# Down projection by seven products: one table for the order of all steps

## The chip, the cores and the metric

The kernel runs on one core of one Trainium2 chip. The metric is the device time of one execution in microseconds. The engines are TensorE (PE in the profile; its weight loads PEld), VectorE (DVE), ScalarE (ACT), GpSimd (POOL) and SyncE (SP), whose queue issues nearly all loads.

## What is computed

Two layers of a trunk over 256 context tokens and 1024 latent tokens. The part that matters here ends each layer, a gated dense network with residual:

```python
h2 = rms_norm(x, norm2_g[l]) * (1.0 + sc2) + sh2
gate, up = jnp.split(h2 @ w_ffn_in[l], 2, axis=-1)
x = x + g2 * ((jax.nn.silu(gate) * up) @ w_ffn_out[l])
```

D_MODEL is 1024 and D_FF 2816. All is float32; the kernel keeps it by splitting each operand into a high and a low part and multiplying three times (low x high, high x low, high x high).

## The kernel before

The tokens stand in three groups `CH`: c = 0, the 256 context tokens, and c = 1 and 2, 512 latent tokens each. The residual is in `xs[c]`, eight tiles of 128 rows. The input of the down projection, 22 tiles of 128 rows, is in DRAM as `FS`, and the projection runs in three parts: four tiles plainly (`ffn_out(0)`, `ffn_out(2)`), sixteen tiles by seven products, and the last two plainly (`ffn_out(NF - 2)`).

The middle part goes through `NC = 4` chunks j of four tiles each. Its 2 x 2 blocks are: two halves of the chunk's rows by the two latent groups on the operand side, two halves of the chunk's rows by two halves of the output rows on the weight side. Seven products replace the eight of the block multiplication: b11, b21, b22 use operands as they are, t1 to t4 use sums of operands, and the weight slabs too are used plainly (`w`) or as sums (`s`). For each chunk there are four slabs m, each giving output tiles m and m + 4; I call one (j, m) a step. A product is six matmuls of 512 columns. The context tokens take an ordinary product (`ctx`, 24 matmuls of 256 columns).

TensorE's order in a step is b21, t2, t1, ctx, t3, b22, then b11 of the next step, then t4. Several products gather in one PSUM bank: b11, t2, t3 and t4 of a step all add to bank a, with an eviction between each two, so t2 may start only when the eviction of b11 has read the bank. Evictions `onto` run on VectorE (five of 512 columns and two of 256 a step), `onto2` on ScalarE (`u`) with the addition to x on GpSimd (two a step).

Beside that run two preparations. For the slabs of the next step (`out_sums`): load to `raw`, split into `w` (ScalarE casts the high part, VectorE subtracts for the low part), form the sums by three GpSimd operations in `raw` itself, split again into `s`. For the next chunk: load b11, b21, b22, c and q (`op_load`, `op_c`), eight operand sums on GpSimd (`op_sum`, into q), splits of the sums tile by tile (`op_t`, operands t1 to t4, each 2 x 128x512) and of the plain operands in place (`op_h`, 128x1024). The operands lie in a ring of 12 places, eight to a chunk, so that some can be written only when the running chunk has last read its own.

The order of all engines in this part is the order in which `out7` issues it, under a manual schedule; what is ahead of it (chunk 0's preparation) is put among the evictions of `ffn_out(2)` by the scheduler. `out7` issues a preparation by `do(at, ...)` at step m = at, and four of them at the first step of the chunk that uses them:

```python
if j and m == 0:
    op_t(j, "t3")
    op_h(j, "b22")
...
if j and m == 0:
    op_t(j, "t4")
```

Of the kernel before, what the change touches and what calls it, by code (L numbers as in the profile page):

```python
# [11 lines left out]
F32 = mybir.dt.float32  # L12
# [7 lines left out]
P = 128  # L20
# [30 lines left out]
def build(tc, d):  # L51
# [60 lines left out]
    queue, ready, steps = [], [], []  # L112
# [62 lines left out]


    def out_sums(src):
        raws = []

        def load():  # L180
            raws.append(raw_slab(src))

        def plain():
            w = wtile()
            split(w[:, 0], w[:, 1], raws[0])
            ready.append(w)
# [7 lines left out]
        def sums_():  # L194
            w = wtile()
            split(w[:, 0], w[:, 1], raws[0])
            ready.append(w)

        steps.append((load, plain, quarters, sums_))

    def want(l):
# [372 lines left out]
    for l in range(DEPTH):  # L574
# [890 lines left out]
        def op_load(j):  # L1465
            f = 4 + 4 * j
            for kind, x, c in (("b11", 0, 1), ("b21", 2, 1), ("b22", 2, 2)):
                ld(operand(j, kind)[:, 1], rows_of(f + x, 2, c))
            qs[j] = [qpool.tile([P, 4, 512], F32, tag="q", bufs=2, name=nm("q")) for _ in range(2)]
            for i in range(2):  # L1470
                nc.sync.dma_start(qs[j][i][:, 0], FS[l][f + i, :, CH[2][0]:])
# [9 lines left out]
        def op_t(j, kind, part=(0, 1)):  # L1481
# [37 lines left out]
        def out1(j, m):  # L1519
            w = ready.pop(0)  # L1520
            pa_ = fpsum(512)
            product(pa_, wq(w, 0), opd(j, "b11"))
            onto(1, m, pa_)
            return w, pa_
# [3 lines left out]
        def out7(j, m, w, pa_):  # L1528
            s_ = ready.pop(0)
            last = (j, m) == (NC - 1, 3)  # L1530
            nj = j + 1 if j + 1 < NC else None
            cur = steps.pop(0) if steps and not last else None

            def do(at, *work):
                if nj and m == at:
                    for x in work:
                        x()

            def ctx():
                pc = psum()  # L1540
# [8 lines left out]
            product(pb, wq(w, 2), opd(j, "b21"))
            if cur:  # L1550
                if steps and (j, m) < (NC - 1, 2):
                    steps[0][0]()
                cur[1]()
            onto(1, m, pb)
            do(0, lambda: op_load(nj))
            product(pa_, wq(s_, 0), opd(j, "t2"), False)
            if cur:
                cur[2]()
            onto2(2, m, pa_)
            product(pc, wq(s_, 3), opd(j, "t1"))  # L1560
            onto(2, m + 4, pc)
            do(1, lambda: op_sum(nj, 1))
            do(2, lambda: op_sum(nj, 4), lambda: op_t(nj, "t2", (0,)))
            do(3, lambda: op_sum(nj, 7))
            if j and m == 0:
                op_t(j, "t3")
                op_h(j, "b22")
            if not last:
                ctx()
            if cur:  # L1570
                cur[3]()
            product(pa_, wq(s_, 1), opd(j, "t3"), False)
            onto2(2, m + 4, pa_)
            do(0, lambda: op_sum(nj, 0))
            do(1, lambda: op_sum(nj, 2), lambda: op_sum(nj, 3))
            do(2, lambda: op_sum(nj, 5), lambda: op_sum(nj, 6))
            do(3, lambda: op_h(nj, "b21"), lambda: op_t(nj, "t1"))
            if j and m == 0:
                op_t(j, "t4")
# [220 lines left out]
```

## Time and profile before

| | us |
|---|---|
| median of 3 runs (3018.08 to 3023.95) | 3021.41 |
| the profiled execution | 3017.62 |
| its span, first to last instruction | 3015.5 |
| TensorE busy | 2871.2 (95%) |
| VectorE / ScalarE / GpSimd busy | 2007.7 / 1210.4 / 998.2 |
| seven-product part, layer 0 (1260.42 to 1479.87) | 219.45 |
| seven-product part, layer 1 (2743.20 to 2964.93) | 221.73 |

In the timeline a row is a run of equal instructions without a gap: start, length, engine, line, operation, output<-inputs, shape, count, and in brackets the idle time just before it with what ended it. A row's length includes the tail of its last instruction, so pitches are read from start to start. Tile names are those of the program: `f` and `ps` are PSUM banks, `ft` the operands, `q` their sums, `raw` the slabs.

### The profile page before, as it was taken

Reading aid. Unit: us, or ns where it says so; the run is one execution under the profiler, and the core shown is the slowest. Engines: PE = TensorE matmul, PEld = TensorE weight load, DVE = VectorE, ACT = ScalarE, POOL = GpSimd, SP = SyncE. Lnnn points to the kernel's source line nnn. Section 1 sums busy time; section 2 is a strip of 40 time slices with the busy share of each in tenths; the row PEclk is TensorE's granted clock in tenths of the full one; section 3 lists DMA queues with packets and bytes.
Section 4 is the critical chain, followed back from the end, with each engine's and each line's share of the span. In section 5 each row is a group of like instructions: output and inputs, shape, how many; then the busy total and the mean of one; then the engine's idle time right before and its main releaser. Section 6 shows DMA issues by size and latency. Waiting matters only on the chain.

```text
span 3015.5 us, 41230 instructions
## 1 busy us (share of the span) xinstructions
PE 2871.2 (95%) x15608; PEld 2452.5 (81%) x15608; DVE 2007.7 (67%) x3157; ACT 1210.4 (40%) x2047; POOL 998.2 (33%) x980
## 2 busy tenths in 40 slices
PE   7999999999999999998999999999999999999997
PEld 4888898888888888877777888888888888887776
DVE  6777787685666554777868677776856533356777
ACT  4523687264223233233442237762622223332342
POOL 1222200035443332376512222001444433315663
PEclk9999999999999999999999999999999999999999
DMA  6576523543333233422235665444434312251212
GB/s 229 155 225 186 175 72 112 180 137 109 124 110 123 91 102 133 147 76 96 91 105 161 206 170 150 107 135 135 149 107 133 101 62 69 69 211 63 91 67 84
DMA packets 164406, 380.63 MB, mean 126 GB/s; under 512 B 20576, under 2 KB 56688, under 8 KB 163952
## 3 DMA queue, kind: packets, MB, share of 16 engines
q1 hardware_dynamic: 119680, 274.00, 29.1%
q0 software_dynamic: 44240, 103.84, 10.2%
q8 instruction: 122, 2.00, 0.3%
q14 instruction: 76, 0.62, 0.1%
q10 hardware_dynamic: 288, 0.16, 0.0%
HBM read 281.97 MB, written 95.95 MB: 125 GB/s over the span
## 4 chain that ended last, share of the span: by engine, by line
PE 66%; DVE 15%; issue 6%; POOL 5%; DMA 4%; ACT 4%; SPq 0%; DVEq 0%; POOLq 0%; ACTq 0%
PE f L1286 30%; PE f L249 15%; PE pa L249 6%; PE pa L489 4%; PE S L429 3%; PE ps L447 3%; DVE w L110 2%; PE ps L249 2%; POOL q L1479 2%; PE ps L967 1%; DVE stt L433 1%; DVE ft L110 1%; DMA x<-XS 1%; ACT E L436 1%; DVE ft L1462 1%
## 5 line engine op out<-in xcount | busy, mean ns | idle before, releaser
L110 DVE TENSOR_TENSOR w<-raw,w 128x1024 fp32r<-128x1024 f32 x278 | 356.2, 1283 | 284.6 <-ACT w L109 284.0
L1286 PE MATMUL f<-h,w 128*128 128x512 f32 x2112 | 506.3, 390 | 1.1 <-ACT pc L1234 1.1
L109 ACT CAST w<-raw 128x1024 fp32r<-128x1024 f32 x278 | 289.8, 1050 | 489.9 <-POOL raw L192 116.6
L1286 PEld LDWEIGHTS f<-h,w 128*128 128x128 f32 x2112 | 392.4, 188 | 82.1 <-ACT pc L1234 1.9
L1286 PE MATMUL f<-ft,w 128*128 128x512 f32 x1344 | 324.5, 396 | 30.3 <-DVE ft L1462 14.8
L1286 PEld LDWEIGHTS f<-ft,w 128*128 128x128 f32 x1344 | 249.6, 190 | 95.0 <-DVE ft L1462 19.9
L1286 PE MATMUL f<-T,w 128*128 128x512 f32 x1080 | 264.8, 394 | 15.0 <-DVE pc L1389 12.0
L1286 PEld LDWEIGHTS f<-T,w 128*128 128x128 f32 x1080 | 201.7, 188 | 65.1 <-DVE pc L1389 16.1
L1227 POOL DMA_DIRECT2D FS<-sg x132 | 72.8, 552 | 541.7 <-DVE sg L1358 222.2
L249 PE MATMUL pa<-h,w 128*128 128x512 f32 (+1 forms) x1296 | 248.4, 352 | 0.8 <-DVE vn L667 0.8
L249 PEld LDWEIGHTS pa<-h,w 128*128 128x128 f32 x1296 | 211.3, 191 | 32.4 <-DVE vn L667 1.0
L489 PE MATMUL pa<-w,h 128*128 128x512 f32 x912 | 218.6, 397 | 12.5 <-DVE w L110 12.0
L433 DVE TENSOR_REDUCE stt<-S 128x1 f32<-128x1280 f32 x128 | 189.9, 1487 | 57.3 <-PE S L429 57.3
L249 PE MATMUL f<-mix,w 128*128 128x512 f32 (+1 forms) x1152 | 225.0, 355 | 0.0
L489 PEld LDWEIGHTS pa<-w,h 128*128 128x128 f32 x912 | 171.9, 191 | 52.8 <-DVE w L110 10.0
L249 PEld LDWEIGHTS f<-mix,w 128*128 128x128 f32 x1152 | 189.8, 189 | 29.5
L436 ACT ACTIVATE E<-S,stt 128x1280 f32<-128x1280 f32 x128 | 170.5, 1332 | 40.9 <-DVE stt L433 40.9
L447 PE MATMUL ps<-vt,pt 128*128 128x128 f32 x1280 | 178.0, 279 | 5.3 <-ACT pt L973 5.2
L249 PE MATMUL f<-ft,w 128*128 128x512 f32 (+1 forms) x864 | 173.7, 362 | 5.7 <-DVE x L1107 5.7
L249 PEld LDWEIGHTS f<-h,w 128*128 128x128 f32 x1392 | 172.7, 192 | 3.3
L249 PE MATMUL f<-h,w 128*128 128x256 f32 x1392 | 174.1, 283 | 0.0
L429 PE MATMUL S<-kb,aq 128*128 128x512 f32 (+1 forms) x624 | 162.7, 377 | 9.7 <-ACT E L436 4.7
(247 smaller groups left out, 4877.4 us busy)
## 6 DMA issues: line engine op xcount, KB each, us to landing
raw<-w_fi SPq DMA_DIRECT2D x112, 512.0 KB, 3.8
ra<-w_adaT SPq DMA_DIRECT2D x96, 256.0 KB, 2.8
FS<-sg POOLq DMA_DIRECT2D x88, 256.0 KB, 2.3
kb<-KS SPq DMA_DIRECT2D x52, 320.0 KB, 6.6
raw<-w_adaT SPq DMA_DIRECT2D x32, 512.0 KB, 4.0
raw<-w_fs SPq DMA_DIRECT2D x32, 512.0 KB, 3.9
ft<-FS SPq DMA_DIRECT2D x32, 512.0 KB, 6.0
raw<-w_in SPq DMA_DIRECT2D x20, 512.0 KB, 3.6
```

Of the source, the lines that this page charges most:

```text
L109: S.copy(hi, src)
L110: V.tensor_sub(lo, src, hi.bitcast(F32))
L249: PE.matmul(ps, lhsT=a, rhs=b, start=(i == 0), stop=(i == n - 1))
L429: PE.matmul(ps[:, o:o + n], lhsT=aq[:, m, q0:q0 + P], rhs=kb[m][1 - p][:, o:o + n], start=(p == 0), stop=(p == 1))
L433: V.reduce_max(st[:, m:m + 1], ps[:, :nkey], axis=AX.X, negate=True)
L436: S.activation(E, ps[:, :nkey], AF.Exp, bias=st[:, m:m + 1], accum_out=st[:, 2 + m:3 + m])
L447: PE.matmul(o[:, :P], lhsT=pt[:, i * P:(i + 1) * P], rhs=vt(b + i), start=(b + i == 0), stop=(b + i == nk - 1))
L489: PE.matmul(ps, lhsT=a[:, y], rhs=wk[:, z], start=(k == 0 and x == 0), stop=(k == KD - 1 and x == 2))
L967: PE.transpose(T_["tp", b][:, x * P:(x + 1) * P], T_["E"][0][:, (4 * b + x) * P:(4 * b + x + 1) * P], ident)
L1227: nc.gpsimd.dma_start(FS[l][f, :, t0:t0 + n], sg)
L1286: PE.matmul(ps, lhsT=y, rhs=z, start=(first and i == 0), stop=(i == 3 * len(a) - 1), skip_group_check=not first)
L1479: G.tensor_sub(q[:, o], x, y)
```

## The change

One table, `PLAN`, has four rows, one for each m, and names every step of every engine in the order in which it is issued. The sign behind a name says for which step or chunk it is: `+` the next step, `++` and `+++` those behind it, `-` the one before; `:` the next chunk, `;` the one after. Names: `ld` load of a slab, `r0` to `r3` its sums, `wa`/`wd` the ScalarE and VectorE halves of the split of the plain slab, `sa`/`sd` of the sums; `P1` to `P5` and `C0`, `C1` VectorE's evictions (`P1` that of b11, ahead of t2), `U2`, `U3` ScalarE's with GpSimd's additions `A2`, `A3`; `b21L` and the like loads, `q0` to `q7` operand sums, `t1a`/`t1d` and `b21a`/`b21d` the ScalarE and VectorE halves of an operand's split.

Slab sums go to a tile `s` of their own (one buffer) in four GpSimd operations of 256 elements, and are made two steps ahead; the raw slab stays whole. An operand sum of both tiles is split at once, 128x1024. q is one tile for both. The buffers of `u` are two in place of four. Loads of b11 and b21 are issued two chunks ahead. The two last w_fo slabs go through the same table, and the last two `tf` tiles are split inside it. TensorE's order is as before, apart from the context product of the very last step.

```diff
-        def quarters():
-            r = raws[0].rearrange("p (q c) -> p q c", q=4)
-            G.tensor_add(r[:, 3], r[:, 1], r[:, 3])
-            G.tensor_sub(r[:, 0:2], r[:, 3:4].to_broadcast([P, 2, 256]), r[:, 0:2])
-            G.tensor_sub(r[:, 1:3], r[:, 1:3], r[:, 0:1].to_broadcast([P, 2, 256]))
...
-            for i in part:
-                split(t[:, 0, i], t[:, 1, i], qs[j][i][:, {"t1": 0, "t3": 1, "t2": 2, "t4": 3}[kind]])
...
+            q = qs[j][:, :, SUMS[kind]]
+            if part == "a":
+                S.copy(t[:, 0], q)
+            else:
+                V.tensor_sub(t[:, 1], q, t[:, 0].bitcast(F32))
...
+        def w_load(g):
+            j, m = divmod(g, 4)
+            raws[g] = raw_slab(d["w_fs"][l, j, m] if j < NC else d["w_fo"][l, (4 + m) * P:(5 + m) * P])
+
+        def w_sum(g, n):
+            if not n:
+                sums_[g] = qpool.tile([P, 4, 256], F32, tag="s", name=nm("s"))
+            r, s_ = raws[g].rearrange("p (q c) -> p q c", q=4), sums_[g]
+            if n == 0:
+                G.tensor_add(s_[:, 3], r[:, 1], r[:, 3])
+            elif n == 1:
+                G.tensor_sub(s_[:, 0], s_[:, 3], r[:, 0])
+            elif n == 2:
+                G.tensor_sub(s_[:, 1], r[:, 0], r[:, 1])
+            else:
+                G.tensor_sub(s_[:, 2], r[:, 2], s_[:, 0])
+
+        def w_split(key, src, part):
+            if part == "a":
+                slabs[key] = wtile()
+                S.copy(slabs[key][:, 0], src)
+            else:
+                V.tensor_sub(slabs[key][:, 1], src, slabs[key][:, 0].bitcast(F32))
...
+        def steps(j, loads=None):
+            for m, names in enumerate(PLAN):
+                for name in names.split():
+                    kind = name.rstrip("+-.:;")
+                    sign = name[len(kind):]
...
+                    g = 4 * j + m + len(sign) * (-1 if "-" in sign else 1)
...
+                    step(kind, g)
...
-        op_load(0)
-        op_c(0)
+        steps(-2, True)
+        steps(-1, True)
         ffn_out(2, fds[1])
...
+        steps(-2, False)
+        steps(-1, False)
+        with tc.manual_schedule():
+            for j in range(NC):
+                steps(j)
...
+    """b21 P1 wa+ P4- r0++ t2a: t2 wd+ q3: t1 P2 U2 ld+++ q7: t2d: cx P5 A2 b21d: r1++ t3 C0 r2++ C1 b22
+    r3++ b22d: U3 A3 b11+ sa++ P3 t4 sd++ cL:""",
```

What the table does to the order, at three places of layer 0. In the names, `x_10332`, `x_10336` and `x_10328` are the residuals of groups 1, 2 and 0, `f_` and `ps_` PSUM banks, `ft_` places of the operand ring, `q_` operand sums, `w_` split slabs.

VectorE before, from the last step of chunk 1 (P3) over the turn to chunk 2 (the second row is P1, the eviction of chunk 2's first b11):

```order
L1506 SCALAR_TENSOR_TENSOR x_10336<-f_11567,mod_83,x_10336 128x512
L1506 SCALAR_TENSOR_TENSOR x_10332<-f_11652,mod_83,x_10332 128x512
L1506 SCALAR_TENSOR_TENSOR x_10332<-f_11548,mod_83,x_10332 128x512
L1462 TENSOR_TENSOR ft_10367<-ft_10367 128x1024
L110 TENSOR_TENSOR w_11679<-raw_11574,w_11679 128x1024
L1506 SCALAR_TENSOR_TENSOR x_10332<-f_11669,mod_83,x_10332 128x512
L1506 SCALAR_TENSOR_TENSOR x_10336<-f_11670,mod_83,x_10336 128x512
L110 TENSOR_TENSOR ft_10367<-q_11270,ft_10367 128x512
L110 TENSOR_TENSOR ft_10367<-q_11271,ft_10367 128x512
L1462 TENSOR_TENSOR ft_10367<-ft_10367 128x1024
```

The splits of c, t3 and b22 stand here behind the turn, inside the step that multiplies by them. VectorE after, the same place:

```order
L1462 TENSOR_TENSOR ft_10367<-q_11273,ft_10367 128x1024
L1511 SCALAR_TENSOR_TENSOR x_10336<-f_11598,mod_83,x_10336 128x512
L1462 TENSOR_TENSOR ft_10370<-q_11273,ft_10370 128x1024
L1469 TENSOR_TENSOR ft_10367<-ft_10367 128x1024
L1511 SCALAR_TENSOR_TENSOR x_10328<-ps_11613,mod_83,x_10328 128x256 x2
L1511 SCALAR_TENSOR_TENSOR x_10336<-f_11598,mod_83,x_10336 128x512
L1462 TENSOR_TENSOR ft_10370<-q_11273,ft_10370 128x1024
L1511 SCALAR_TENSOR_TENSOR x_10332<-f_11661,mod_83,x_10332 128x512
L1511 SCALAR_TENSOR_TENSOR x_10332<-f_11556,mod_83,x_10332 128x512
L1497 TENSOR_TENSOR w_11670<-s_11582,w_11670 128x1024
```

Now t3, t1, c and t4 (the four rows that write `ft_`) are split ahead of P1 of the next chunk (the third row from the end), and behind it only slabs are.

VectorE before, in step m = 2 of chunk 1, from P2 to P1 of the next step:

```order
L1506 SCALAR_TENSOR_TENSOR x_10332<-f_11462,mod_83,x_10332 128x512
L1506 SCALAR_TENSOR_TENSOR x_10336<-f_11463,mod_83,x_10336 128x512
L110 TENSOR_TENSOR ft_10367<-q_11270,ft_10367 128x512
L1506 SCALAR_TENSOR_TENSOR x_10328<-ps_11498,mod_83,x_10328 128x256 x2
L110 TENSOR_TENSOR w_11525<-raw_11373,w_11525 128x1024
L1506 SCALAR_TENSOR_TENSOR x_10336<-f_11463,mod_83,x_10336 128x512
L1462 TENSOR_TENSOR ft_10369<-ft_10369 128x1024
L1506 SCALAR_TENSOR_TENSOR x_10332<-f_11548,mod_83,x_10332 128x512
```

P1, the last row, stands behind the split of b11 of the next chunk. VectorE after, the same step:

```order
L1511 SCALAR_TENSOR_TENSOR x_10332<-f_11471,mod_83,x_10332 128x512
L1462 TENSOR_TENSOR ft_10367<-q_11273,ft_10367 128x1024
L1511 SCALAR_TENSOR_TENSOR x_10336<-f_11493,mod_83,x_10336 128x512
L1469 TENSOR_TENSOR ft_10369<-ft_10369 128x1024
L1511 SCALAR_TENSOR_TENSOR x_10328<-ps_11507,mod_83,x_10328 128x256 x2
L1469 TENSOR_TENSOR ft_10367<-ft_10367 128x1024
L1511 SCALAR_TENSOR_TENSOR x_10336<-f_11493,mod_83,x_10336 128x512
L1497 TENSOR_TENSOR w_11563<-s_11482,w_11563 128x1024
L1511 SCALAR_TENSOR_TENSOR x_10332<-f_11556,mod_83,x_10332 128x512
```

Now P1 stands behind the split of the slab sums of two steps ahead (sd), and the step splits three whole operands, t2, b21 and b22.

GpSimd before, in step m = 2 of chunk 1 (the sums of the next slab, additions to x and operand sums):

```order
L190 TENSOR_TENSOR raw_11373<-raw_11373 128x256
L191 TENSOR_TENSOR raw_11373<-raw_11373 128x512
L192 TENSOR_TENSOR raw_11373<-raw_11373 128x512
L1512 TENSOR_TENSOR x_10336<-x_10336,u_11485 128x512
L1479 TENSOR_TENSOR q_11271<-ft_10367,q_11271 128x512
L1512 TENSOR_TENSOR x_10336<-x_10336,u_11534 128x512
L1479 TENSOR_TENSOR q_11271<-q_11271,ft_10369 128x512
L1479 TENSOR_TENSOR q_11271<-ft_10367,q_11271 128x512
```

The slab's sums are one block, in the slab itself. GpSimd after, the same step:

```order
L1484 TENSOR_TENSOR s_11482<-raw_11402 128x256
L1452 TENSOR_TENSOR q_11273<-ft_10369,q_11273 128x512 x2
L1586 TENSOR_TENSOR x_10336<-x_10336,u_11501 128x512
L1486 TENSOR_TENSOR s_11482<-s_11482,raw_11402 128x256
L1488 TENSOR_TENSOR s_11482<-raw_11402 128x256
L1490 TENSOR_TENSOR s_11482<-raw_11402,s_11482 128x256
L1586 TENSOR_TENSOR x_10336<-x_10336,u_11553 128x512
```

Now they are four short operations of the slab two steps ahead, with two operand sums and an addition between them; one operand sum fewer stands in this step and one more in the step ahead of it.

## Rows read from the trace of the kernel before

**Rows 1.** Busy us (count) by stretch: PE, PEld, DVE, ACT, POOL; granted clock, DMA share, GB/s.

```profile
1260.42:1316.68 56.26, 53.45 (x277) 44.87 (x276) 35.26 (x45) 19.14 (x24) 36.20 (x28) 1.00 0.32 109
1316.68:1373.45 56.77, 52.43 (x264) 43.70 (x264) 40.84 (x49) 21.55 (x28) 39.66 (x28) 0.97 0.25 86
1373.45:1429.95 56.50, 51.28 (x264) 42.57 (x264) 41.34 (x49) 21.51 (x28) 39.74 (x28) 1.00 0.22 76
1429.95:1479.87 49.92, 48.02 (x253) 40.66 (x254) 38.64 (x44) 19.06 (x23) 23.68 (x17) 1.00 0.22 68
...
2743.20:2964.93 221.73, 205.71 (x1058) 171.81 (x1056) 157.26 (x186) 80.17 (x102) 138.53 (x101) 0.99 0.24 80
...
1200.00:1230.00 30.00, 30.00 (x158) 25.79 (x157) 21.99 (x31) 9.44 (x10) 4.08 (x4) 1.00 0.91 341
```

**Rows 2.** Timeline of PE in the first chunk of layer 0, undisturbed.

```profile
1266.29 3.04 PE L249 MATMUL ps<-ft,w 128*128 128x256 f32 x24
1269.16 9.71 PE L1286 MATMUL f<-ft,w 128*128 128x512 f32 x42
1278.70 3.04 PE L249 MATMUL ps<-ft,w 128*128 128x256 f32 x24
```

**Rows 3.** Timeline of PE at the turn from the second chunk to the third.

```profile
1357.89 3.06 PE L1286 MATMUL f<-ft,w 128*128 128x512 f32 x12 [0.93 <-DVE x L1506]
...
1370.93 1.43 PE L1286 MATMUL f<-ft,w 128*128 128x512 f32 x5 [1.42 <-DVE ft L1462]
...
1383.06 8.38 PE L1286 MATMUL f<-ft,w 128*128 128x512 f32 x35 [1.27 <-DVE ft L1462]
```

**Rows 4.** PE's waits in 1260.42 to 1479.87: us in total, times, longest.

```profile
PE f L1286 <- DVE ft L1462: 7.7, 6, 1.5
PE f L1286 <- DVE x L1506: 5.1, 5, 1.1
PE f L1286 <- DVE ft L110: 1.1, 2, 0.5
```

**Rows 5.** Timeline of DVE, POOL and ACT in layer 0's part.

```profile
1355.95 1.23 DVE L1462 TENSOR_TENSOR ft<-ft 128x1024 fp32r<-128x1024 f32 x1 [2.21 <-POOL q L1479]
1357.09 0.74 DVE L1506 SCALAR_TENSOR_TENSOR x<-f,mod,x 128x512 f32<-128x512 f32 x1
...
1336.28 1.29 POOL L192 TENSOR_TENSOR raw<-raw 128x512 f32<-128x512 f32 x1
1337.61 1.06 ACT L109 CAST w<-raw 128x1024 fp32r<-128x1024 f32 x1 [3.40 <-POOL raw L192]
1338.70 1.23 DVE L110 TENSOR_TENSOR w<-raw,w 128x1024 fp32r<-128x1024 f32 x1
1338.78 2.30 POOL L1479 TENSOR_TENSOR q<-q,ft 128x512 f32<-128x512 f32 x1
```

**Rows 6.** One stretch by tile: raw, q (DVE, ACT, POOL), u (ACT, POOL), line L1462 (DVE).

```profile
1388.34:1414.82 26.48, 5.72 (x4) 3.15 (x3) 6.95 (x6) 1.00 0.25 82
...
1388.34:1414.82 26.48, 0.73 (x1) 0.61 (x1) 12.83 (x7) 1.00 0.25 82
...
1388.34:1414.82 26.48, 2.76 (x4) 5.16 (x4) 1.00 0.25 82
...
1388.34:1414.82 26.48, 1.23 (x1) 1.00 0.25 82
```

**Rows 7.** POOL's groups in 1260.42 to 1479.87: busy us, mean ns, idle before, releaser.

```profile
L1512 POOL TENSOR_TENSOR x<-x,u 128x512 f32<-128x512 f32 x32 | 44.3, 1384 | 18.4 <-ACT u L1511 18.4
...
L190 POOL TENSOR_TENSOR raw<-raw 128x256 f32<-128x256 f32 x15 | 11.1, 738 | 51.0 <-DVE w L110 51.0
```

**Rows 8.** Timeline of SP's queue ahead of the x loads of layer 0.

```profile
1188.87 0.33 SPq L105 DMA_DIRECT2D raw<-w_fo  x1
1196.38 0.33 SPq L105 DMA_DIRECT2D raw<-w_fs  x1
```

**Rows 9.** PE's waits in 1199 to 1260.42, as in rows 4.

```profile
PE f L249 <- DVE x L1107: 2.9, 2, 2.1
```

More of the change, by code (lines that the diff above doesn't have):

```diff
@@ L110, in split @@
         V.tensor_sub(lo, src, hi.bitcast(F32))
-    queue, ready, steps = [], [], []
+    queue, ready = [], []
     pools = {}
@@ L1462, in halve, with op_load, q_load @@
             V.tensor_sub(t[:, 1], t[:, 1].bitcast(F32), t[:, 0].bitcast(F32))
[L1465 to L1471, printed above, removed]
+        HALVES = {"b11": (0, 2, 1), "b21": (2, 2, 1), "b22": (2, 2, 2), "c": (0, 4, 0)}
+        SUMS = {"t1": 0, "t3": 1, "t2": 2, "t4": 3}
+        def op_load(j, kind):
+            x, n, c = HALVES[kind]
+            ld(operand(j, kind)[:, 1], rows_of(4 + 4 * j + x, n, c))
+        def q_load(j, i):
+            if not i:
+                qs[j] = qpool.tile([P, 2, 4, 512], F32, tag="q", name=nm("q"))
+            nc.sync.dma_start(qs[j][:, i, 0], FS[l][4 + 4 * j + i, :, CH[2][0]:])
         def op_sum(j, n):
             i, n = divmod(n, 4)
-            q = qs[j][i]
+            q = qs[j][:, i]
             b11, b21, b22 = (ops[j, k][:, 1, i].bitcast(F32) for k in ("b11", "b21", "b22"))
@@ L1517, in opd @@
             return [(t[:, 0, i], t[:, 1, i]) for i in range(2)]
[L1519 to L1540, printed above, removed]
+        banks = {}
@@ L1549, in out7 @@
[L1549 to L1579, printed above, removed]
-            product(pc, wq(s_, 2), opd(j, "b22"), False)
-            onto(2, m, pc)
-            do(2, lambda: op_h(nj, "b11"))
-            nxt = None
-            if last:
-                ctx()
-            else:
-                nxt = out1(j, m + 1) if m < 3 else out1(nj, 0)
-            do(2, lambda: op_c(nj), lambda: op_t(nj, "t2", (1,)))
@@ L1656, in build @@
         ffn_out(0, fds[0])
-        op_load(0)
-        op_c(0)
+        steps(-2, True)
+        steps(-1, True)
         ffn_out(2, fds[1])
-        for n in range(8):
-            op_sum(0, n)
-        for kind in ("b11", "b21", "t2", "t1", "c", "t3", "b22", "t4"):
-            (op_t if kind[0] == "t" else op_h)(0, kind)
-        for x in steps.pop(0):
-            x()
-        steps[0][0]()
-        nxt = out1(0, 0)
-        man = ExitStack()
-        man.enter_context(tc.manual_schedule())
-        for j in range(NC):
-            for m in range(4):
-                nxt = out7(j, m, *nxt)
-            if j == NC - 2:
-                for x in range(2):
-                    ld(tf[:, x, 1], FS[l][NF - 2 + x])
-        man.close()
+        steps(-2, False)
[3 more added lines that the diff above has]
+                steps(j)
+            for m, names in enumerate(PLAN):
+                for name in names.split():
+                    if name[-1] == "-" and m < name.count("-"):
+                        step(name.rstrip("-"), 4 * NC + m - name.count("-"))
+        ready.extend(slabs["f", x] for x in range(2))
         fts = [tf[:, x] for x in range(2)]
-        for x in fts:
-            halve(x)
         dq.close()
```

142 lines of the change are left out of this document (110 added, 32 removed).

## The prediction

> **What bounds the kernel now.** I began with the stage that the change touches: the down projection by seven products, once per layer. The table of busy time by stretch [rows 1] cuts it into its four chunks. In layer 0 they take 56.26, 56.77, 56.50 and 49.92 us, together 219.45; the whole stage of layer 1 takes 221.73. Next I asked for TensorE's own timeline. Where nothing stops it [rows 2], 42 matmuls of 512 columns (seven products) go from 1269.16 to 1278.70, 9.54 us or 1.363 per product, and the context product from 1266.29 to 1269.16, 2.87. One step (chunk j, slab m) is therefore 12.41 us at least, a chunk 49.6, and the sixteen steps of a stage 198.6. The change leaves the matmuls as they are, so 198.6 is a floor, and what can be won is 219.45 - 198.6 = 20.9 in layer 0 and 221.73 - 198.6 = 23.1 in layer 1, 44.0 in all. The fourth chunk stands at its floor already; all of the excess lies in the first three.
>
> Where it lies there: at the turn from one chunk to the next TensorE stops four or five times [rows 3]. Product t2 waits for VectorE's eviction of the product before it from the same bank (1357.89). Others wait for an operand that is still being split (1370.93, 1383.06). The list of waits over the stage [rows 4] names the same three: 7.7, 5.1 and 1.1 us, all on VectorE. The rest of the 20.9 is the clock (the second chunk's granted clock is 0.97 on average [rows 1], some of it at the lower of the two levels, 1.2 in place of 2.4 GHz: 0.03 x 56.77 = 1.7 us are lost) and the gaps of some tenths of a microsecond around each stop.
>
> Why VectorE is late: it isn't short of time (41.34 of 56.50 us in the third chunk [rows 1]), it waits in its queue. At 1355.95 the split of b21 has stood idle 2.21 us for a GpSimd sum that reads b21, and the eviction behind it starts at 1357.09 only [rows 5]; t2 follows at 1357.89. And the splits of t3 and b22 are written in the code after the step m = 0 that uses them has begun.
>
> **The change, part by part.** *Order of the operand work.* The splits of b11, b21, b22, t2, t1, t3 and c of the next chunk all stand ahead of the turn in the table, and t4 at the very end of m = 3, a step before its use. The waits for operands (7.7 + 1.1 [rows 4]) then have no cause. *Splits of both tiles at once.* Eight 128x512 splits (0.73 us for the one in [rows 6]) become four 128x1024 at 1.23 [rows 5]: 5.84 to 4.92 us of VectorE per chunk. *Slab sums in a place of their own.* Three GpSimd operations (0.73 + 1.29 + 1.29) become four of 256 elements, 2.92 us in place of 3.31. More important, before, the first of them overwrites the raw slab and must wait for the slab's plain split: GpSimd sat idle 51.0 us of the stage there [rows 7]. That wait goes, and sums are made two slabs ahead. *Evictions* (28 per chunk of VectorE, 8 of ScalarE and GpSimd) stay as they are, as does the last step apart from its context product, which moves up two places.
>
> *The new queueing.* What is late next? VectorE and GpSimd get in each other's way. At 1338.70 a split of 1.23 us runs, and the GpSimd operation that starts 0.08 later takes 2.30 in place of 1.29 [rows 5]; beside evictions, whose first input is in PSUM, I found no such lengthening. So I add for each step what VectorE's operations with two SBUF inputs and GpSimd's would take one after the other. GpSimd has per step 2.92 of sums and 2.58 of additions to x, and of the eight operand sums (1.29) two, four, two, none; VectorE has 3, 3, 5, 5 splits of 1.23:
>
> m = 0: 8.08 + 3.69 = 11.77. m = 1: 10.66 + 3.69 = 14.35. m = 2: 8.08 + 6.15 = 14.23. m = 3: 5.50 + 6.15 = 11.65. Chunk: 52.0, against 49.6 of TensorE.
>
> How much of this fits into a microsecond is read from the busiest stretch of before, 1388.34 to 1414.82, where TensorE stood only at the very end [rows 6]. GpSimd did 17 operations (two of them short: 2 x 0.73 + 15 x 1.29 = 20.81), VectorE 5 x 1.23 + 0.73 = 6.88; together 27.69 us of work in 26.48, or 1.046 per us. GpSimd was idle 1.6 us of it; without these it is 27.69 / 24.84 = 1.115. A whole chunk (52.0 / 49.6 = 1.048) thus just fits. But steps m = 1 and 2 bring 28.58 in a time of 24.82. At 1.046 that needs 27.3, 2.5 too much; at 1.115 it needs 25.6, 0.8 too much. This lateness reaches TensorE by one way: r3 (last slab sum) - sa (ScalarE's half of the split) - sd (VectorE's half) - P1, the eviction behind sd in VectorE's queue - t2 of the next step. Undisturbed, b22 ends 9.68 into a step, sa takes 1.06 more [rows 5], sd 1.23, P1 0.74, so P1 is done at 12.71; t2 wants it at 12.41 + 1.36 = 13.77. Slack 1.06. The stall is then 2.5 - 1.06 = 1.4 or nothing (0.8 < 1.06), once per chunk, and is worked off in m = 3 and 0. I take 1.0, nearer to the first, since GpSimd also waits in order for ScalarE's u (18.4 us of a stage before [rows 7]). Chunks 0 to 2: 50.6; chunk 3, with no operand sums: 49.6; stage 201.4. Gain 219.45 - 201.4 = 18.0 and 221.73 - 201.4 = 20.3; sum 38.3.
>
> This is the place for a rule. In [rows 5] the two operations of 1.23 and 1.29 were over 2.38 us after the first began, not 2.52, so the trace nearly serialises them. The Trainium skill, "SBUF — State Buffer", section "SBUF: two separate sides", says that a GpSimd operation and a VectorE operation with two SBUF inputs exclude each other for the whole instruction. By that rule a chunk could never be under 52.0, a stage would be 205.6, and the gain 30.0; the trace differs by the 1.046 per us above, 5% past what the rule allows, and decides.
>
> *Loads and what lies before the stage.* The order of SP's queue changes: b11 and b21 of chunk 1 (512 KB each) are issued before the x loads, in a gap in which SP stood still anyway, from 1188.87 to 1196.38 [rows 8]. Cost nothing; if that cover were gone, 1 MB more ahead of x costs some 3 us per layer (x and its neighbours moved at 341 GB/s in 1200 to 1230 [rows 1]). The operand work of chunk 0 is still scheduled among the evictions of the product before it, where TensorE waits 2.9 us [rows 9]; the sums that these splits wait for are as many and start on the same load, so I leave it at 2.9, with ends of 0 and 5.8: 3 us per layer either way. What follows the stage I leave as it is. The stretch at the lower clock came after the stage's first stalls, and the third and fourth chunks, with stalls as long, show 1.00; I count it gone. If it stays, it costs 1.7 us per layer.
>
> **The rivals.**
> 1. *All of it is hidden.* GpSimd is always ready and the 1.115 holds; stages at 198.6, gain 44.0, 2977.4. For: 51 us of GpSimd's idle time go. Against: the local 28.58 in 24.82.
> 2. *Strict exclusion*, two-input operations of VectorE and GpSimd never beside each other at all: chunks 52.0, stage 3 x 52.0 + 49.6 = 205.6, gain 30.0, 2991.4. For: 2.30 in place of 1.29. Against: 27.69 in 26.48. (It is the rule named above.)
> 3. *The pair does no better than it did over whole chunks.* Before, a chunk held 12 x 1.23 + 8 x 0.73 + 4 x 0.73 + 24 x 1.29 = 54.5 in 56.50, 0.964 per us. At that rate 52.0 needs 53.9, a stage is 211.3, the gain 18.6: 3002.8. Against: at the turns of before it was the order that held both.
> 4. *Slower.* The stall sits in every step, not once a chunk: the sums have a single tile, so r0 of the next slab waits for sd, and lateness passes from step to step along r3 - sa - sd - P1. Slower from 44.0 / 32 = 1.4 us per step. At 2.2 (m = 1 and 2 overfull by 1.9 and 1.8, and none of it worked off) it would be 70 us of stalls: 3048. Against: m = 0 and 3 have room, 11.8 and 11.7 against 12.4.
> 5. *It doesn't do what it says*: the turns keep their waits because the loads of the next chunk (b22, q, c) come late behind SP's waits for slabs. Gain under 6. Against: the table issues each a half step (6 us) or more before the first instruction that reads it.
>
> **How the numbers follow.** The profiled execution took 3017.62 us, 2.1 more than its span, and lies 3.8 below the median of 3021.41. All terms are differences within the trace, so I take them from the median: 3021.4 - 38.3 = 2983.1. Forecast 0.50, own range 2978 to 2991 (a stall of 0 to 2.4 per chunk). Rivals: all hidden 0.20, strict 0.12, no better than before 0.10, slower 0.05, no effect 0.03. The range leaves out the slower case, the no-effect case and the edges: 2975 (all hidden with 2.5 won before the stage) to 3003. A measurement of this kernel can tell about 0.2%, 6 us, from no change. Faster by more 0.91, within 0.03, slower 0.06.
>
> **What would show it.** Right: the list of waits of TensorE in the stage has no operand splits any more, and one wait of about 1 us per chunk for the eviction P1, at t2 of step m = 3; GpSimd's first slab sum has lost its idle time; stages of 200 to 203 us. Rival 2 or 3: VectorE's splits and GpSimd's operations lengthen further than 1.3 to 1.8 us, with stalls at most steps m = 2 and 3. Wrong: TensorE waiting for ScalarE's u or a slab split, for operand loads, or more than 6 us before the stage.

## The result and the profile after

The changed kernel takes **2982.27 us** (median of 4 runs, 2981.57 to 2983.71); the kernel before, on the same chip, 3022.52 (3018.08 to 3023.95). The ratio is 0.987, with a 95% interval of 0.9853 to 0.9887: faster by 1.3%, clear of the noise. The forecast was 2983.1, with a range of 2975 to 3003.

The profiled execution took 2982.61 us, 35.0 less than the profiled execution of before; its span is 2980.8, 34.7 less. Its stages first. The view is the table of busy time by stretch, as in [rows 1]: the four chunks of layer 0, then the whole stage of layer 1.

```profile
1260.96:1310.35 49.39, 49.13 (x260) 41.81 (x259) 40.09 (x44) 20.15 (x23) 39.67 (x32) 1.00 0.24 74
1310.35:1360.74 50.39, 50.15 (x266) 42.88 (x265) 40.66 (x45) 21.62 (x24) 41.52 (x33) 1.00 0.29 95
1360.74:1411.11 50.37, 50.13 (x266) 42.88 (x265) 40.63 (x45) 21.63 (x24) 41.46 (x33) 1.00 0.27 85
1411.11:1463.53 52.42, 51.53 (x271) 43.89 (x270) 31.95 (x42) 18.29 (x20) 18.73 (x17) 1.00 0.22 76
2726.59:2929.23 202.64, 200.98 (x1058) 171.46 (x1056) 153.15 (x172) 80.65 (x90) 140.18 (x112) 1.00 0.24 77
```

The stages take 202.57 and 202.64 us (forecast 201.4; before 219.45 and 221.73). The gains are 16.9 and 19.1, together 36.0. Before, the first three windows were the long ones; now it is the fourth. The windows are not cut at whole chunks, though, which have 264 matmuls: the fourth here holds 271, seven or some 1.6 us more, and the fourth of [rows 1] 253, some 2.5 us fewer, so that two stops of the kernel before lie inside that one (TensorE's timeline):

```profile
1437.32 0.96 PE L1286 MATMUL f<-ft,w 128*128 128x512 f32 x3 [0.55 <-DVE ft L110]
1439.55 8.66 PE L1286 MATMUL f<-ft,w 128*128 128x512 f32 x35 [1.27 <-DVE ft L1462]
```

Below, steps are compared instead. The granted clock is 1.00 in all of them, so the stretch at the lower level is gone, as I had counted.

TensorE's waits: first those of layer 0's stage, which answer to [rows 4] (layer 1 has the same line), then those before it, which answer to [rows 9].

```profile
PE f L1255 <- DVE x L1511: 1.6, 5, 0.5
...
PE f L218 <- DVE x L1076: 1.8, 2, 1.4
```

No operand split is named any more; the only wait is the one for an eviction. Before the stage 1.8 us are left of 2.9. Line numbers have moved: 1255 is the product (1286 before), 1511 the eviction (1506), 218 the other matmuls (249).

GpSimd's groups in layer 0's stage, as in [rows 7] (busy us, mean ns, idle before, releaser):

```profile
L1586 POOL TENSOR_TENSOR x<-x,u 128x512 f32<-128x512 f32 x32 | 47.8, 1494 | 34.3 <-ACT u L1583 34.3
...
L1486 POOL TENSOR_TENSOR s<-s,raw 128x256 f32<-128x256 f32 x14 | 18.5, 1319 | 0.9
...
L1484 POOL TENSOR_TENSOR s<-raw 128x256 f32<-128x256 f32 x14 | 10.3, 738 | 34.4 <-DVE w L1497 34.4
```

The 51.0 us of idle time ahead of the first slab sum have not gone, they became 34.4: it now waits for the single tile `s`, until VectorE has split the sums in it. But the wait costs nothing now: the kernel with both late edits, near the end of the experiments, idles 37.3 us at the same place of layer 0's stage, and TensorE doesn't wait in that stage at all.

In what follows a step is measured from the start of one context product to the start of the next: 15 steps of a stage, whose floor is 186.3 us (189.0 where the last context product stands two products later, as in the old frame). What a kernel takes above the floor is its **excess**. Before: 20.3 and 21.0 us in the two layers. After: 3.9 and 3.9, of which in layer 0 0.9 lie in the first chunk, 0.7 each in the second and third (at the ends of steps m = 1 and 2, ahead of t2 of the next step), and 1.5 in the fourth (0.78 and 0.72).

### The profile page after: what moved, and what is told of

Read it like the earlier page. It is cut to its first block, busy times and chain, and to the rows that moved or that the text cites. A ratio compares the mean times of both kernels' runs of the same rounds, so it can differ in the third digit from the quotient of the medians.

```text
span 2980.8 us, 41280 instructions
## 1 busy us (share of the span) xinstructions
PE 2867.1 (96%) x15608; PEld 2454.1 (82%) x15608; DVE 2004.4 (67%) x3125; ACT 1210.3 (41%) x2015; POOL 1008.2 (34%) x1012
## 4 chain that ended last, share of the span: by engine, by line
PE 69%; DVE 13%; POOL 6%; issue 5%; ACT 4%; DMA 3%; SPq 0%; DVEq 0%; ACTq 0%; POOLq 0%
PE f L1255 28%; PE f L218 18%; PE pa L218 6%; PE pa L458 4%; PE ps L416 4%; PE S L398 4%; PE ps L218 2%; POOL q L1452 2%; PE ps L936 2%; DVE stt L402 1%; DVE w L110 1%; ACT E L405 1%; POOL x L1586 1%; DVE ps L275 1%; DMA raw<-w_adaT 1%
## 5 line engine op out<-in xcount | busy, mean ns | idle before, releaser
L110 DVE TENSOR_TENSOR w<-raw,w 128x1024 fp32r<-128x1024 f32 x210 | 265.5, 1266 | 270.3 <-ACT w L109 269.8
L109 ACT CAST w<-raw 128x1024 fp32r<-128x1024 f32 x210 | 218.4, 1050 | 356.2 <-POOL raw L159 107.3
L1255 PE MATMUL f<-ft,w 128*128 128x512 f32 x1344 | 315.5, 391 | 3.3 <-DVE x L1511 3.1
L1255 PEld LDWEIGHTS f<-T,w 128*128 128x128 f32 x1080 | 201.7, 188 | 65.4 <-DVE pc L1358 16.1
```

The lines of the kernel that those rows point to most:

```text
L109: S.copy(hi, src)
L110: V.tensor_sub(lo, src, hi.bitcast(F32))
L1255: PE.matmul(ps, lhsT=y, rhs=z, start=(first and i == 0), stop=(i == 3 * len(a) - 1), skip_group_check=not first)
```

## Experiments

**Which part of the change pays?** Two kernels each make one part in the code of before, and one makes both. In the first the slab sums get a tile of their own and become four short operations, in the old order:

```diff
-            G.tensor_add(r[:, 3], r[:, 1], r[:, 3])
...
+            s_ = pools["s"].tile([P, 4, 256], F32, tag="s", name=nm("s"))
+            G.tensor_add(s_[:, 3], r[:, 1], r[:, 3])
...
-            t = qpool.tile([P, 512], F32, tag="u", bufs=4, name=nm("u"))
+            t = qpool.tile([P, 512], F32, tag="u", bufs=2, name=nm("u"))
```

> The kernel before with one part of the change alone: slab sums in a tile of their own (four short GpSimd operations, u with two buffers), everything in the old order. If the order of the operand splits is what pays (my theory), the turns keep their stops and at most the wait of P1 behind a split that waits for GpSimd shrinks: 3012 to 3022. If it is the 51 us of GpSimd's idle time, that is the in-place sums, that held the kernel before: 2992 or less.

Measured: 2995.43 us, ratio 0.9911 (0.9896 to 0.9925); 27.7 us below before. My expectation fell, and the other one (2992 or less) was nearly reached. Excess 8.1 and 8.3. The tile, the shorter operations (2.92 us a step in place of 3.31) and the two buffers of `u` in place of four were not tried apart from each other.

In the second the operand sums and splits move to the steps in which the table has them, and the slab sums stay in the slab:

```diff
-            do(2, lambda: op_sum(nj, 4), lambda: op_t(nj, "t2", (0,)))
-            do(3, lambda: op_sum(nj, 7))
-            if j and m == 0:
-                op_t(j, "t3")
-                op_h(j, "b22")
+            do(1, lambda: op_sum(nj, 1), lambda: op_sum(nj, 5))
+            do(2, lambda: op_t(nj, "t2"))
+            do(3, lambda: op_t(nj, "t3"))
...
-            do(2, lambda: op_sum(nj, 5), lambda: op_sum(nj, 6))
-            do(3, lambda: op_h(nj, "b21"), lambda: op_t(nj, "t1"))
-            if j and m == 0:
-                op_t(j, "t4")
+            do(1, lambda: op_sum(nj, 2))
+            do(2, lambda: op_h(nj, "b21"))
+            do(3, lambda: op_t(nj, "t1"), lambda: op_h(nj, "c"))
...
```

> The kernel before with the operand work alone put where the table has it (operand sums 2, 4, 2, 0 in steps m = 0 to 3; b11 in m = 1; t2, b21, b22 in m = 2; t3, t1, c, t4 in m = 3), slab sums still in place and one step ahead, splits still tile by tile. My theory: most of the 40 us, 2986 to 3000, with what remains as waits for P1, since the two-input work of VectorE and GpSimd is 54.5 per chunk in place of 52.0. If the sums' own place is needed: 3010 or more.

Measured: 3014.21 us, ratio 0.9974 (0.9963 to 0.9985). Excess 17.5 and 16.1. This fell too, and the other expectation (3010 or more) came: where I had put nearly all of the gain there are 9 us. The waits of TensorE, VectorE and GpSimd in layer 0's stage:

```profile
PE f L1286 <- DVE x L1506: 9.7, 8, 2.3
PE f L1286 <- ACT u L1511: 3.1, 3, 1.1
...
DVE w L110 <- ACT w L109: 12.5, 9, 2.8
...
POOL raw L190 <- DVE w L110: 55.1, 12, 6.7
```

The order alone does take away TensorE's waits for operand splits (7.7 + 1.1 us in [rows 4]). But GpSimd still stands 55.1 us ahead of its first slab sum, VectorE 12.5 us at slab splits, and TensorE now waits 9.7 us for evictions in place of 5.1, and 3.1 us for ScalarE's `u`.

> The two parts of e1_own_place and e2_order together. What then separates it from the changed kernel is the split of both tiles at once and that slab sums are one step ahead in place of two. My theory: 2982 to 2990. If the early slab sums carry a part: 2992 to 3005.

Measured: 3006.27 us, ratio 0.9949 (0.9934 to 0.9964); excess 14.5 and 14.1. Both parts together are worse than the first alone, and past both expectations. So the parts don't add up, and "the order" is not one thing. Three traces say what happens. The first lines below are those of the kernel with the own place alone, in layer 0: GpSimd's first slab sum, VectorE's waits for operand sums, and TensorE's waits.

```profile
L192 POOL TENSOR_TENSOR s<-raw 128x256 f32<-128x256 f32 x14 | 15.6, 1117 | 0.0
...
DVE ft L1466 <- POOL q L1483: 3.7, 3, 1.2
...
PE f L1289 <- DVE x L1510: 5.0, 3, 1.7
PE f L1289 <- DVE ft L110: 0.2, 1, 0.2
```

GpSimd no longer idles before a slab sum (51.0 us in [rows 7]); its operand sums come earlier, and VectorE waits 3.7 us for them in place of 9.3 in the stage of before, where [rows 5] show one such wait:

```profile
DVE ft L1462 <- POOL q L1479: 9.3, 6, 2.2
```

TensorE is left with one stop of 1.7 us per turn. The late splits of t3 and b22, written behind the turn, cost 0.2 us in all in that order: they had been late because GpSimd was.

With both parts, the end of step m = 2 looks like this (timeline of layer 0; in the last row TensorE). The slab sums start at 1347.08, behind a run of four operand sums:

```profile
1347.08 1.19 POOL L192 TENSOR_TENSOR s<-raw 128x256 f32<-128x256 f32 x1
...
1350.83 1.05 ACT L109 CAST w<-s 128x1024 fp32r<-128x1024 f32 x1 [4.34 <-POOL s L195]
...
1351.91 1.23 DVE L110 TENSOR_TENSOR w<-s,w 128x1024 fp32r<-128x1024 f32 x1 [2.10 <-ACT w L109]
...
1353.44 1.94 DVE L1466 TENSOR_TENSOR ft<-ft 128x1024 fp32r<-128x1024 f32 x1 [0.30 <-ACT ft L1465]
...
1355.96 1.21 DVE L1466 TENSOR_TENSOR ft<-ft 128x1024 fp32r<-128x1024 f32 x1
...
1357.09 1.39 DVE L1510 SCALAR_TENSOR_TENSOR x<-f,mod,x 128x512 f32<-128x512 f32 x2
...
1357.88 4.62 PE L1289 MATMUL f<-ft,w 128*128 128x512 f32 x12 [2.16 <-DVE x L1510]
```

VectorE stands 2.10 us at the split of the slab sums; behind it in its queue are the splits of b21 and b22 and only then P1 (1357.09), for which t2 waits.

I took that for the cause, and moved the split of the slab sums to the end of the step in this kernel, behind the splits of b21 and b22:

```diff
-            if cur:
-                cur[3]()
...
             do(2, lambda: op_h(nj, "b22"))
+            if cur:
+                cur[3]()
             nxt = None
```

> The combination of the two parts in the old frame (3006.27, step m = 2 stops 2.0 to 2.3 us at t2 of the next step), with one thing moved: both halves of the split of the slab sums go from the middle of the step (behind the context product) to its end, behind the operand splits of the step and ahead of P1. Theory: in the combination VectorE takes that split first, stands 2.10 us for it, and the two operand splits and P1 queue up behind; with the late one last the stop of step m = 2 falls under 1, three times 1.3 to 2.2 us in each of two stages, and the time to 2991 to 2999. Rival: the slab sums themselves are late (GpSimd takes the operand sums first), so the order on VectorE moves the wait without shortening it: 3003 to 3009.

Measured: 3016.03 us, ratio 0.9986 (0.9976 to 0.9996), excess 18.3 in both layers: 10 us worse, and past the rival's figures too. VectorE and ScalarE in the same place:

```profile
1355.38 0.69 ACT L1515 ACTIVATE u<-f,mod 128x512 f32<-128x512 f32 x1 [3.93 <-PE f L1289]
...
1355.96 1.99 ACT L1465 CAST ft<-ft 128x1024 fp32r<-128x1024 f32 x2
1357.09 2.06 DVE L1466 TENSOR_TENSOR ft<-ft 128x1024 fp32r<-128x1024 f32 x1 [2.03 <-POOL x L1516]
```

VectorE now stands at b21's split. GpSimd's addition is named, but ScalarE's halves of the splits of b21 and b22 (1355.96) fit better: the first of the two ends about 1 us in, at 1357. They had stood behind the eviction U3, for whose product ScalarE waited 3.93 us. The stop only changed its place in the queues.

**What of the table makes the difference?** Four of the things that set the changed kernel apart from the kernel with both parts were each taken back alone. Splits of t tile by tile, 128x512 again:

```diff
-                V.tensor_sub(t[:, 1], q, t[:, 0].bitcast(F32))
+                    V.tensor_sub(t[:, 1, i], q, t[:, 0, i].bitcast(F32))
```

> The changed kernel with one part undone: the splits of t1 to t4 tile by tile again (eight of 128x512 in place of four of 128x1024). It adds 0.9 us of VectorE's two-input work per chunk, in steps m = 2 and 3. My theory: it adds to the lateness of P1 at m = 3, 0.2 to 0.9 us per chunk, 2983 to 2988. Rival, that VectorE has room for it: 2982.

Measured: 2986.31 us (2983.25 to 2988.4), 4.0 more than after; the steps that end in m = 3 lengthen from 12.9 or 13.0 us to between 13.2 and 13.7, and the excess is 5.6 and 6.5 in place of 3.9. That is as expected: 0.92 us more of VectorE's work per chunk, on the chain to P1.

Slab sums and splits one step ahead in place of two (`r0++` becomes `r0+` and so on, at the same places; `sd+` of the next chunk's first step moves from behind t2 to the end of m = 3):

```diff
-    b11+ sa++ A3 P3 t4 sd++ q6:""",
+    b11+ sa+ A3 P3 t4 sd+ q6:""",
...
-    b11L; b22 U3 b21L; C0 C1 A3 b11+ P3 t4a: sa++ t4 t4d:""",
+    b11L; b22 U3 b21L; C0 C1 A3 b11+ P3 t4a: sa+ t4 sd+ t4d:""",
```

> The changed kernel with the slab sums and their splits one step ahead in place of two, at the same places of the table (only in the last step of a chunk the second half of the split moves up from behind t2 of the next step). Theory: two steps ahead buy nothing, since with one tile for the sums the chain r3, sa, sd, P1 is the same; 2979 to 2986. Rival: the distance is what lets the crowded steps pass; t2 then waits for its slab at every step, 2990 to 3020.

Measured: 2988.04 us, ratio 0.9894 (0.9879 to 0.9909), 6 more than after and between the two expectations. Away from the turn the distance is worth nothing here: no step there is longer than in the changed kernel. The stop is at the turn (steps of 13.8 us in place of 12.42), and it is the one line that had to move:

```profile
1362.67 1.23 DVE L1497 TENSOR_TENSOR w<-s,w 128x1024 fp32r<-128x1024 f32 x1 [1.22 <-ACT w L1495]
1363.81 1.22 DVE L1462 TENSOR_TENSOR ft<-q,ft 128x1024 fp32r<-128x1024 f32 x1
...
1364.95 2.06 DVE L1511 SCALAR_TENSOR_TENSOR x<-f,mod,x 128x512 f32<-128x512 f32 x3
...
1365.75 3.02 PE L1255 MATMUL f<-ft,w 128*128 128x512 f32 x12 [1.07 <-DVE x L1511]
```

VectorE stands 1.22 us at that split, t4's split and P1 behind it, and TensorE stops for 1.07.

ScalarE's halves of the splits of b21 and b22 back from m = 0 to m = 2, next to VectorE's:

```diff
-    """b21 b11a: P1 qL0: qL1: b22L: P4- wa+ t2 sd+ b21a: t1 P2 r0++ U2 wd+ r1++ cx A2 P5 ld+++ b22a: r2++
+    """b21 b11a: P1 qL0: qL1: b22L: P4- wa+ t2 sd+ t1 P2 r0++ U2 wd+ r1++ cx A2 P5 ld+++ r2++
...
+    r3++ b22a: b22d: U3 A3 b11+ sa++ P3 t4 sd++ cL:""",
```

> The changed kernel with ScalarE's halves of the splits of b21 and b22 moved from step m = 0 to a place right ahead of their VectorE halves in m = 2; nothing else. Theory: ScalarE's lead of two steps is what the old frame lacks (there, in the combination with the split last, the split of b21 on VectorE stood 2.03 us until ScalarE, which works in order behind a u, had done its half); VectorE then waits in m = 2 ahead of P1, the stop at t2 of m = 3 grows from 0.5 to 1.5 to 2.5, and the time to 2989 to 2997. Rival: ScalarE has room there, and the lead is worth nothing: 2980 to 2986.

Measured: 2983.20 us (2981.47 to 2984.32); no change, and the waits of TensorE are the same 1.6 us. In this frame the lead is worth nothing. Here both halves still stand ahead of U3, though; what the halves behind U3 would cost in this frame was not tried.

GpSimd's order in steps m = 1 and 2 as in the old frame, the four slab sums in one block:

```diff
-    """b21 P1 q1: wa+ P4- t2 wd+ r0++ t1 r1++ P2 U2 ld+++ r2++ cx A2 P5 r3++ q5: t3 C0 C1 q2: b22 b11d: U3
...
+    """b21 P1 wa+ P4- t2 wd+ r0++ r1++ r2++ r3++ t1 P2 U2 q1: q5: ld+++ cx A2 P5 t3 C0 C1 q2: b22 b11d: U3 q6:
...
-    """b21 P1 wa+ P4- r0++ t2a: t2 wd+ q3: t1 P2 U2 ld+++ q7: t2d: cx P5 A2 b21d: r1++ t3 C0 r2++ C1 b22
...
+    """b21 P1 wa+ P4- t2a: q3: q7: t2 wd+ r0++ r1++ r2++ r3++ t1 P2 U2 ld+++ t2d: cx P5 A2 b21d: t3 C0 C1 b22
```

> The changed kernel with GpSimd's order in m = 1 and 2 as in the old frame: the four sums of a slab as one block behind t2, the operand sums two by two (in m = 2 both ahead of the block, in m = 1 behind it). The same work in each step. Theory: with ScalarE's halves ahead and the slab's split last, GpSimd's order within a step matters little: 2980 to 2990. Rival: it is this interleaving that keeps the slab sums in time; then stops of about 2 us at t2 of m = 3, as in the combination in the old frame, 2994 to 3006.

Measured: 2983.33 us (2981.19 to 2986.38): no change by the time either, and an excess of 4.6 and 4.5 in place of 3.9.

**What holds the last 3.9 us per stage?** The prediction named the chain r3, sa, sd, P1, t2. It is seen in the changed kernel at the end of m = 2 (timeline of all engines, layer 0):

```profile
1347.35 1.73 POOL L1490 TENSOR_TENSOR s<-raw,s 128x256 f32<-128x256 f32 x1
...
1349.11 1.06 ACT L1495 CAST w<-s 128x1024 fp32r<-128x1024 f32 x1 [1.87 <-POOL s L1490]
1350.20 1.23 DVE L1497 TENSOR_TENSOR w<-s,w 128x1024 fp32r<-128x1024 f32 x1 [1.06 <-ACT w L1495]
...
1351.34 1.41 DVE L1511 SCALAR_TENSOR_TENSOR x<-f,mod,x 128x512 f32<-128x512 f32 x2
...
1352.14 1.66 PE L1255 MATMUL f<-ft,w 128*128 128x512 f32 x6 [0.24 <-DVE x L1511]
```

Each row starts as the one before it ends; r3 took 1.73 us in place of 0.73, beside VectorE's split of 1346.81. In the last chunk, which has no operand sums, another row stands ahead of P1:

```profile
1438.33 1.49 DVE L1431 TENSOR_TENSOR ft<-ft 128x1280 fp32r<-128x1280 f32 x1
1439.74 1.40 DVE L1511 SCALAR_TENSOR_TENSOR x<-f,mod,x 128x512 f32<-128x512 f32 x2
1440.54 1.66 PE L1255 MATMUL f<-ft,w 128*128 128x512 f32 x6 [0.46 <-DVE x L1511]
```

It is the split of a `tf` tile, of 1280 elements, at the end of steps m = 1 and 2. Two edits take one cause each, and a third kernel has both. The splits of `tf` move behind P5 of the next step:

```diff
+                    if j == NC - 1 and m > 1 and kind == "P5":
+                        halve(tf[:, m - 2])
...
-                    elif m < 3:
-                        halve(tf[:, m - 1])
```

> The changed kernel with the two splits of the last plain operands (128x1280) moved from the ends of steps m = 1 and 2 of the last chunk, where they stand ahead of P1, to the place behind P5 in steps m = 2 and 3, where VectorE waits for the context product anyway. Theory: they are the cause of the two stops of the last chunk, 0.8 and 0.7 us per layer: 3.0 us less, 2979. Rival, that P1 is late there for another reason: 2982.

P1 goes ahead of sd, which moves into the next step:

```diff
...
-    b11+ sa++ A3 P3 t4 sd++ q6:""",
...
+    b11+ sa++ A3 P3 t4 q6:""",
...
-    """b21 P1 wa+ P4- r0++ t2a: t2 wd+ q3: t1 P2 U2 ld+++ q7: t2d: cx P5 A2 b21d: r1++ t3 C0 r2++ C1 b22
...
+    """b21 P1 sd+ wa+ P4- r0++ t2a: t2 wd+ q3: t1 P2 U2 ld+++ q7: t2d: cx P5 A2 b21d: r1++ t3 C0 r2++ C1 b22
...
```

> The changed kernel with the table changed at one point: P1 stands ahead of sd, the VectorE half of the split of the slab sums, in steps m = 1, 2 and 3 (sd moves one step later). Theory: the chain last slab sum - sa - sd - P1 - t2 makes the stop at t2 of m = 2 and 3 (0.2 and 0.5 us per chunk) and adds to those of the last chunk: 4 to 7 us less, 2975 to 2978. Rival, that VectorE is late at P1 by its own work (three whole operands split in m = 2): 2982.

> The edits of e4_tf_late and e6_p1_first together. Theory: nothing stands ahead of P1 any more; stages at 199 to 200 us, 2974 to 2977. If the stops have another cause: 2979 to 2982.

Measured: the `tf` splits alone 2981.68 us (2975.69 to 2982.5), P1 first 2977.21 (2973.86 to 2978.84), both 2974.10 (2972.03 to 2976.28), ratio 0.9845 (0.9831 to 0.9858). The first is too small to be told from no change by the time; by the trace the two stops of the last chunk are gone (steps of 12.42). With P1 first all stops ahead of t2 go but those two. With both, TensorE has no wait in either stage. The 15 steps of the two stages there (busy time by stretch):

```profile
1265.77:1452.07 186.30, 186.30 (x992) 161.40 (x990) 143.50 (x160) 74.52 (x84) 132.57 (x110) 1.00 0.27 84
2726.97:2913.26 186.29, 186.29 (x991) 161.38 (x990) 141.99 (x160) 74.61 (x84) 134.03 (x110) 1.00 0.26 81
```

That is the floor, twice; 2 x 3.9 = 7.8 us were to be had, and 8.2 came. This version beats both kernels.

**Is the pair VectorE and GpSimd really full?** The changed kernel with six of the eight operand sums of a chunk done twice, 6 x 1.29 = 7.74 us more of GpSimd's work per chunk, 46.4 us in all:

```diff
-            G.tensor_sub(q[:, o], x, y)
+            for _ in range(2 if j and n != 1 else 1):
+                G.tensor_sub(q[:, o], x, y)
```

> The changed kernel with six of the eight operand sums of chunks 1 to 3 done twice (the second writes the same values): 6 x 1.29 = 7.7 us more of GpSimd per chunk, 59.7 of two-input work against 52.0. At the 1.046 per us read before, a chunk is 57.1, at 1.115 it is 53.5, in place of the 50.4 measured: 19 to 40 us more, 3001 to 3022. Strict exclusion: 59.7, 56 us more, 3038. If the two engines do not bind each other and GpSimd has room (41.5 of 50.4 us busy): 2982 to 2988.

Measured: 3039.57 us, ratio 1.0057 (1.0043 to 1.0071), 57.3 us more than after, past my range. The excess is 32.5 and 32.3. Rows of layer 0 (all engines), around the stop ahead of t2 of step m = 3 in the second chunk, and one of TensorE in the first:

```profile
1355.93 6.13 POOL L1453 TENSOR_TENSOR q<-ft,q 128x512 f32<-128x512 f32 x4
...
1356.38 1.92 DVE L1463 TENSOR_TENSOR ft<-q,ft 128x1024 fp32r<-128x1024 f32 x1 [1.60 <-ACT ft L1461]
...
1362.09 2.29 DVE L1470 TENSOR_TENSOR ft<-ft 128x1024 fp32r<-128x1024 f32 x1 [3.13 <-POOL q L1453]
...
1310.37 5.09 PE L1255 MATMUL f<-ft,w 128*128 128x512 f32 x12 [5.64 <-DVE x L1512]
```

The steps of the first chunk lengthen by 1.6 and 8.7 us over the floor, at the ends of m = 1 and 2. Of the 8.7 some 2 are the clock: the 12 matmuls behind the stop of 5.64 us have a pitch of 4.92 us to the next product (1310.37 to 1315.29) in place of 2.87, with a granted clock of 0.54 there. Without it, and without the 0.7 that a chunk stopped before, 7.5 us reached TensorE. That is all of what was added. For a row's length includes a tail, which the next instruction overlaps, and of two sums that nothing disturbs the second starts 1.25 us after the first (2.54 - 1.29, here in the kernel with the split at the end):

```profile
1340.11 2.54 POOL L1483 TENSOR_TENSOR q<-q,ft 128x512 f32<-128x512 f32 x2
```

6 x 1.25 = 7.5. So at this place there is no room left, though GpSimd is busy for only 160 of 219 us. Two sums were added in each of the steps m = 0, 1 and 2, and step m = 3, which has room, doesn't help: VectorE holds the split of b21 until GpSimd is through (3.13 us above), and P1 stands behind it.

The time is near the 3038 of strict exclusion, but by chance: that figure has row lengths for work and leaves out the clock, which is some 12 of the 57 us. The rows speak better for it. What stands behind an undisturbed split starts 1.14 us after it (1362.67, 1363.81 and 1364.95 above), so four sums and one split are 4 x 1.25 + 1.14 = 6.14 us from start to start, and they were over in 6.13: they took turns. Only by row lengths, 4 x 1.29 + 1.23 = 6.39, do the two engines seem to run beside each other, here as in [rows 6]. The Trainium skill, "SBUF — State Buffer", section "SBUF: two separate sides", has the two exclude each other for the whole instruction; these rows agree, with 6.13 us against 6.14.

## Why the prediction was right, and where it was not

The time was right, 2982.27 against 2983.1. Step by step:

- *Floor of 198.6 and at most 44.0 to win*: right. The version with both late edits stands on the floor. *All of the excess in the first three chunks, the fourth at its floor*: misread. The fourth's window is eleven matmuls short, and the step with the two stops shown above is 2.8 us over its floor. The 44.0 doesn't hang on it.
- *Waits for operands go*: right, none is left. *Because of the order*: wrong as the main cause of the gain. I had read the turns as a matter of where the splits are written, and gave the 51.0 us of GpSimd's idle time no number of its own. The order alone takes the waits for operands away too, but most of the time goes to other waits, and 9 us are won; the own place alone leaves 0.2 us of them and wins 27.7.
- *GpSimd's idle time before the first slab sum goes*: wrong, it is 34.4 of 51.0, now for the single tile. I had named that wait under the slower rival; it costs nothing, as the version on the floor shows, which has 37.3.
- *A stop of 1.0 per chunk in chunks 0 to 2, on the chain r3, sa, sd, P1, t2*: the chain is right, shown by the kernel that puts P1 first. The size was 0.9, 0.7 and 0.7 and not 1.0, and only 0.5 of each stands at t2 of m = 3, the rest one or two steps ahead of it.
- *52.0 us of paired work per chunk, 1.046 of it in a microsecond, so 5% past exclusion*: misread. I added row lengths. From start to start (1.25 and 1.14 us, and 0.69 and 0.60 for the short ones, read the same way) the stretch of [rows 6] holds 15 x 1.25 + 2 x 0.69 + 5 x 1.14 + 0.60 = 26.4 us in 26.48, and the two operations of [rows 5] are 2.39 in 2.38: turns, with nothing to spare. Steps m = 1 and 2 then bring 27.1 in 24.82, 2.3 too much, near the 2.5 that I had, because the lengths and the rate erred the same way. The lighter end, 1.115, falls with the lengths; and GpSimd's idle time there was 1.9 us by its busy time, not 1.6.
- *Chunk 3 at its floor, since it has no operand sums*: wrong by 1.5 us. The diff moves the splits of the last two `tf` tiles into this chunk; I described that and did not cost it, though each is 1.49 us of VectorE ahead of P1, more than the slack of 1.06 that I had worked out. Stage together: 3.9 above the floor, forecast 3.0.
- *Nothing before the stage*: wrong by 3.4 us in the good sense. The product ahead of it went from 60.41 to 58.02 and from 58.69 to 57.70 us; the waits left, 1.8 and 1.5, lie within the ends that I gave. 1.3 of the 2.4 us in layer 0 are the clock behind the wait, which I hadn't counted: its 96 matmuls had a granted clock of 0.92 before and 1.00 after.
- *The sum*: 36.0 of the stages and 3.4 before them are 39.4, forecast 38.3. The two errors nearly cancel, so it is luck in part that the time came within 1 us. The spans differ by only 34.7, since all other code took 4.7 us more than in the profiled execution of before, 2.9 of them in the first 200 us, whose code the change leaves as it was; that execution lay 3.8 below its median. Against the medians (40.25) the sum stands as it was made.
- *Rivals*: all hidden (2977.4) is the kernel with the late splits moved, not this one. The times of strict exclusion (2991.4), no better than before (3002.8), slower (3048) and no effect didn't come. But strict exclusion was priced too high: from start to start a chunk holds 49.3 us of paired work, not 52.0, and so the time doesn't speak against it.

What stays open: why both parts in the old frame are worse than one. The rows show each stop there as a split that stands at the head of VectorE's queue and waits, with P1 behind it; none of the four things taken back alone in the changed kernel brings those stops back in full. So it is several of them together, or one of the things that were not taken back (the order of the loads, the single tile q, the places of ScalarE's other halves and of the evictions); neither was tried.

## What to carry to other kernels

When an engine waits in its queue, ask first who made its input late: here VectorE's late splits were a symptom of GpSimd, which idled 51 us behind a buffer it wanted to overwrite, and a buffer of its own, with slightly shorter sums, paid three times as much as a new order. The idle time is no measure by itself: the version on the floor idles 37 us at the same place, when nothing that is due stands behind it. Then look, in every queue, at what stands ahead of the one instruction that the critical engine waits for: the same split costs nothing behind P1 and a stop ahead of it, and the two moves of that kind won the last 8 us. Two good edits can be worth less together than one alone, so measure them apart and together before crediting either.

## What the runs showed of the hardware

A stop of 5.64 us of TensorE was paid twice: the 12 matmuls behind it took 4.92 us at the lower clock (granted 0.54) in place of 2.87. Shorter stops went both ways. In the kernel with both parts the row at 1357.88 shows 4.62 us for its 12 matmuls behind 2.16, and in the one with the split at the end 12 matmuls behind 2.08 showed 3.01. In the kernel before, 12 matmuls took 4.43 us behind stops of 1.46 and 1.10 (at 1316.68), and 3.02 behind stops of 1.42 and 1.10 (at 1373.45). So the length of the stop alone doesn't decide it; what else does was not looked into.

VectorE's splits and GpSimd's sums took turns: four sums and one split, 6.14 us from start to start, were over in 6.13, and 26.4 us of such work filled 26.48. What was added to GpSimd where this was full, 7.5 us a chunk, reached TensorE in full.
